# Score tiles of two attentions given the first rank in an instruction planner, and no planned distance between their steps on one engine

## The chip, the cores and the metric

The kernel runs on one core of a Trainium2 chip. A core has five engines that work side by side, each through its own instructions in a fixed order: TensorE (PE, matrix products and transposes into PSUM), VectorE (DVE), ScalarE (ACT), GpSimd (POOL), and SyncE (SP), which here issues nearly all DMAs. They wait for one another through semaphores. The metric is the device time of one execution in microseconds (us), as the median of several runs.

## The reference

One layer of a hybrid encoder on 272 tokens (16 learned meta tokens and 256 of input) of 2048 channels, in float32:

```python
hn = rmsnorm(h, mix_norm_g[l])
q_a, k_a, v_a, cq, ckv, k_pe = jnp.split(hn @ w_in[l], IN_SPLITS, axis=-1)
out_a = neighbourhood_attention(rmsnorm(q_a), rmsnorm(k_a), v_a, rpb, meta_bias)     # 8 heads of 128
out_b = mla_attention(cq, ckv, k_pe, ..., w_q_up, w_kv_up, ...)                       # 8 heads of 128 + 64
mix = jnp.concatenate([rmsnorm(out_a), rmsnorm(out_b)], axis=-1)
h = h + mix @ w_out[l]
h = h + conv_glu(rmsnorm(h), w_gate[l], w_up[l], conv_w[l], conv_b[l], w_down[l])    # width 5632
```

(The norms' gains are left out in this sketch.) Both attentions take a softmax over keys. In group A a token sees its neighbourhood on a grid and the meta tokens, with a learned bias and a mask added to the scores; in group B it sees all tokens, and queries and keys come from low-rank latents by further projections and carry a rotary part.

## The kernel before

**Precision and weights.** A float32 product is made of three products of a faster kind: each operand is split into a high and a low half, `hi = round(x)` on ACT and `lo = x - hi` on DVE. All weights pass through this: a DMA on SP brings a piece of up to 1024 columns into one of five `raw` tiles, ACT writes `whi`, DVE writes `wlo` (512 columns at a time), and PE multiplies by them (`mm3`, L595: three matmuls a block, lines L598 to L600). So PE, ACT and DVE all work for the stream of weights the whole time.

**Attention stage.** Heads are taken in four pairs. For each pair the weight stream on PE makes, in the order of `ORDERS`, the latent attention's queries and keys (Q, K), the neighbourhood attention's queries and keys (q, k), and the values of both (V, v), into four PSUM banks called `acc`. Around it other work runs: `na_queries`, `na_keys`, `na_values` and their `mla_` counterparts read those banks (which frees them), normalise and split; when queries and keys of a head are there, `na_head` (L1228) or `mla_head` (L1444) starts two *score tiles* of 128 queries by 272 keys each, `na_tile` (L1177) or `mla_tile` (L1389), 32 in all. A tile's steps are:

- score matmuls on PE (three, or five with the rotary part) into one of two PSUM banks `sps`;
- neighbourhood: scale and bias on DVE (STT, which frees the bank), row maximum on DVE (RED, L261); latent: row maximum on DVE, its product with the query's scale on DVE (`cols<-cols,rq`);
- exponential with row sum on ACT (`p<-...`; in the latent attention this frees the bank);
- reciprocal (L265) and normalisation (L249) on DVE, a copy of the 16 meta columns on ACT and its low half on DVE (`p<-p`);
- three transposes on PE into one of two banks `tps` (L287), which ACT and DVE split into `pt`.

The head then multiplies by the values (`attend`, L1020). Key sums of squares, small sums and `attend` take banks of `sps` too. After the fourth pair come the output projection and the gated MLP.

**The planner.** The order of the instructions on each engine is found when the program is built, by a list scheduler, `Flow` (L105). All work is written as threads, Python generators that yield the engine and an estimated cost of each step, wait for an `Event`, or ask for tiles from `Slots` (first come, first served). `Flow.run` (L187) again and again takes, of all threads' next steps, the one with the least

```python
key = (start, th.order(), th.seq)      # start = max(clock[eng], th.t + latency(th, eng))
```

and emits its instructions. `th.t` is when the thread's previous step ends by the plan. So the rank (`order`, the thread's `prio`, or its value when it is a function) decides among steps with one start, as all have that wait for a busy engine; less is earlier. `latency` (L114) is the distance planned between two steps of a thread: 700 to 1000 ns towards PE (`TO_PE`, `SMALL_PE`), 200 from it, 140 otherwise (`OTHER`). It is 0 where both steps are PE's, and, for threads whose `prio` is a function or at least 2, where both are on one engine. Threads are started by `fl.spawn(gen, prio=0)` (L127). The weight stream on PE has rank 1, the halves of the weights rank 2 (-1 while fewer than two pieces are ready), and nearly all others 0, among which the one spawned first goes first.

The chip's engines keep the planned order, while real times differ from the plan: an instruction whose operands are late holds up all behind it on its engine.

Of the kernel before, what the change touches and what calls it, by code (L numbers as in the profile page):

```python
# [83 lines left out]
class Event:  # L84
    def __init__(self):
        self.time, self.waiting, self.src = None, [], None
# [6 lines left out]
        self.free, self.waiting = [(0.0, t) for t in tiles], []  # L93


class Thread:
    def __init__(self, gen, t, prio, seq):
        self.gen, self.t, self.eng, self.prio, self.seq, self.req = gen, t, None, prio, seq, None
# [6 lines left out]
class Flow:  # L105
# [8 lines left out]
    def latency(self, th, eng):  # L114
        if th.eng == eng and (eng == "pe" or callable(th.prio) or th.prio >= 2):
            return 0.0
        if eng == "pe":
            if th.src == "pool":
                return self.POOL_PE
            return self.SMALL_PE if th.prio == 0 and not self.crowded else self.TO_PE  # L120
        return self.FROM_PE if th.eng == "pe" else self.OTHER

    def __init__(self):
# [85 lines left out]
def encoder_block(ctx: ExitStack, tc: tile.TileContext, io):  # L209
    nc = tc.nc  # L210
    ctx.enter_context(tc.manual_schedule())
    fl = Flow()
# [24 lines left out]
    def ACT(out, in_, f, **kw):  # L237
        ns = (51 if in_psum(in_) else 93) + 0.833 * size(in_)
        ns += 93 * (columns(kw.get("scale")) + columns(kw.get("bias")) > 0)
        yield "act", ns + 113 * ("accum_out" in kw)  # L240
        nc.scalar.activation(out, in_, f, **kw)  # L241

    def TT(out, a, b, op):
        yield "dve", 68 + 1.04 * size(out)
        nc.vector.tensor_tensor(out, a, b, op)  # L245

    def TS(out, a, s0, s1, *ops):
        yield "dve", 68 + 62 * columns(s0, s1) + (1.04 if in_psum(a) else 0.52) * size(out)
        nc.vector.tensor_scalar(out, a, s0, s1, *ops)  # L249

    def STT(out, a, s, b, op0, op1):
        yield "dve", 68 + 62 * columns(s) + 1.04 * size(out)
        nc.vector.scalar_tensor_tensor(out, a, s, b, op0, op1)  # L253
# [5 lines left out]
    def RED(out, a, op, **kw):  # L259
        yield "dve", 68 + 1.04 * size(a)  # L260
        nc.vector.tensor_reduce(out, a, AX.X, op, **kw)  # L261

    def RECIP(out, a):
        yield "dve", 75
        nc.vector.reciprocal(out, a)  # L265
# [11 lines left out]
    def MM(items):  # L277

        yield "pe", sum(cost(l, r) for _, l, r, _, _ in items)
        for o, l, r, start, stop in items:  # L280
            nc.tensor.matmul(o, l, r, start=start, stop=stop)  # L281
# [7 lines left out]
    def meta_copies(row, lo, n=P):  # L289

        out = row[:n, L : L + 3 * CW].rearrange("p (i x) -> p i x", i=3)[:, :, :N_META]
        src = row[:n, SEQ:L]
        his = out[:, :2] if lo == 2 else out[:, ::2]
        yield from ACT(his.bitcast(F32R), repeated(src, 2), AF.Copy)
        yield from TT(out[:, lo].bitcast(F32R), src, out[:, 0], ALU.subtract)
# [4 lines left out]
    def one(slots):  # L300
        (t,) = yield slots, 1
        return t
# [182 lines left out]
    def load(out, src, ev, queue):  # L485

        nc_bytes = 4 * P * size(out)
        t = max(dma_free[0], fl.cur.t) + nc_bytes / (290.0 if fl.crowded else 350.0)
        dma_free[0] = t
        queue.dma_start(out, src)  # L490
        fl.set(ev, t + (2200.0 if fl.crowded else 2000.0) - fl.cur.t)
# [504 lines left out]
    def product3(out, ls, rs, start, stop):  # L996
        (lh, ll), (rh, rl) = ls, rs
        return [(out, lh, rh, start, False), (out, lh, rl, False, False), (out, ll, rh, False, stop)]
# [13 lines left out]
    def p_transposed(p, PT, q0):  # L1012
        pt = yield from one(tps)
        yield from chunks_transposed(p, pt)
        fl.put(probs, p)
        src = pt[:, : 3 * P].rearrange("p (c q) -> p c q", c=3)
        yield from split_chunks(PT[:, :, q0 : q0 + P], src)
        fl.put(tps, pt)
# [158 lines left out]
    def na_tile(s, c, i, B, PT, done):  # L1177
        sb = yield from one(scr)
        w = yield from one(cols)
        S = yield from one(sps)  # L1180
        q0 = i * P
        k, q = s.k[c], slice(q0, q0 + P)
        yield from MM(
            product3(
                S[:, :L], (s.q[:, c, 0, q], s.q[:, c, 1, q]), (k[:, 0], k[:, 1]), True, True
            )
        )
        j = 2 * c + i
        yield from STT(sb[:, :L], S[:, :L], s.rq[:, j : j + 1], B[:, i, :], ALU.mult, ALU.add)
        fl.put(sps, S)  # L1190
        yield from RED(w[:, 0:1], sb[:, :L], ALU.max, negate=True)
        p = yield from one(probs)
        yield from ACT(p[:, :L], sb[:, :L], AF.Exp, bias=w[:, 0:1], accum_out=w[:, 1:2])
        fl.put(scr, sb)
        yield from RECIP(w[:, 2:3], w[:, 1:2])
        yield from TS(p[:, :L], p[:, :L], w[:, 2:3], None, ALU.mult)
        fl.put(cols, w)
        yield from meta_copies(p, 1)
        yield from p_transposed(p, PT[:, c], q0)
        fl.set(done)  # L1200
# [27 lines left out]
    def na_head(s, pr, c):  # L1228
        h = 2 * pr + c
        B = yield from one(bias)  # L1230
        yield "sp", 600
        ev_B = Event()
        load(B, io["na_bias"][h], ev_B, nc.sync)
        yield s.ev_q
        yield s.ev_k[c]
        yield ev_B
        if c == 0:
            s.PT = yield from one(pts)
            fl.set(s.ev_PT)
        yield s.ev_PT  # L1240
        done = [Event() for _ in range(2)]
        for i in range(2):
            fl.spawn(na_tile(s, c, i, B, s.PT, done[i]))
        if c == 1:
            fl.spawn(na_small(s, pr, s.PT, s.ev_few))
        for ev in done:
            yield ev
        fl.put(bias, B)
        yield s.ev_few
        fl.put(na_k, s.k[c])  # L1250
        s.left += 1
        if s.left == 2:
            fl.put(na_q, s.q)
            fl.put(qss, s.qs)
            fl.put(rq6, s.rq)
        yield s.ev_v[c]
        if h:
            yield ev_oa[h - 1]
        yield from attend(s.V[c], s.PT[:, c], SEQ, "g_oa", h, oa[h], sum_a, ev_oa[h])
        fl.put(na_v, s.V[c])  # L1260
        if c == 1:
            fl.put(pts, s.PT)
# [126 lines left out]
    def mla_tile(s, c, i, PT, done):  # L1389
        w = yield from one(cols)  # L1390
        p = yield from one(probs)
        S = yield from one(sps)
        S_ = S[:, :L]
        q0 = i * P
        q = slice(q0, q0 + P)
        k, kp = s.k[c], s.kp[c]
        yield from MM(
            product3(S_, (s.q[:, c, 0, q], s.q[:, c, 1, q]), (k[:, 0, :], k[:, 1, :]), True, False)
            + [(S_, s.qr[:, c, 0, q], kp, False, False), (S_, s.qr[:, c, 1, q], kp, False, True)]
        )  # L1400
        j = 2 * c + i
        rq = s.rq[:, j : j + 1]
        yield from RED(w[:, 0:1], S_, ALU.max, negate=True)
        yield from TT(w[:, 3:4], w[:, 0:1], rq, ALU.mult)
        yield from ACT(p[:, :L], S_, AF.Exp, bias=w[:, 3:4], scale=rq, accum_out=w[:, 1:2])
        fl.put(sps, S)
        yield from RECIP(w[:, 2:3], w[:, 1:2])
        yield from TS(p[:, :L], p[:, :L], w[:, 2:3], None, ALU.mult)
        fl.put(cols, w)
        yield from meta_copies(p, 1)  # L1410
        yield from p_transposed(p, PT[:, c], q0)
        fl.set(done)
# [31 lines left out]
    def mla_head(s, pr, c):  # L1444
        h = 2 * pr + c
        yield s.ev_q
        yield s.ev_qr
        yield s.ev_k[c]
        if c == 0:
            s.PT = yield from one(pts)  # L1450
            fl.set(s.ev_PT)
        yield s.ev_PT
        done = [Event() for _ in range(2)]
        for i in range(2):
            fl.spawn(mla_tile(s, c, i, s.PT, done[i]))
        if c == 1:
            fl.spawn(mla_small(s, s.PT, s.ev_few))
        for ev in done:
            yield ev
        yield s.ev_few  # L1460
        fl.put(mk, s.k[c])
        fl.put(mkp, s.kp[c])
        s.left += 1
        if s.left == 2:
            fl.put(mq, s.q)
            fl.put(mqr, s.qr)
            fl.put(qss, s.qs)
            fl.put(rq6, s.rq)
        yield s.ev_v
        if h:  # L1470
            yield ev_ob[h - 1]
        d = slice(c * P, (c + 1) * P)
        yield from attend(s.V[:, :, d], s.PT[:, c], NT, "g_ob", h, ob[h], sum_b, ev_ob[h])
        s.left_v += 1
        if s.left_v == 2:
            fl.put(mv, s.V)
            fl.put(pts, s.PT)
# [713 lines left out]
```

## Time and profile before

| | |
|---|---|
| median of 3 runs | 1108.5 us (1107.95 to 1108.92) |
| profiled execution | 1108.39 us |
| its span, first to last instruction | 1106.6 us |
| busy: PE, DVE, ACT, POOL | 1099.4, 1000.6, 726.9, 171.5 us |
| granted TensorE clock | 1.000 |
| attention tiles at work | about 84 to 284 us |

A busy engine is one with an instruction in execution. Matmuls overlap one another, so their durations add up to more than the busy time; how far apart two of them start tells what one costs. Waits in square brackets name the instruction whose semaphore came last. Lines like L245 (`TT`) or L241 (`ACT`) are those of helpers, so instructions are told apart by the tiles that they write and read.

### The profile page before, as it was taken

The numbers are of one execution on the slowest core, as the hardware profiler recorded it, in microseconds if no ns is written. First come the engines' busy times: TensorE is split into PE (matmuls) and PEld (weight loads), VectorE is DVE, ScalarE is ACT, GpSimd is POOL, SyncE is SP. The second block draws the span as 40 slices with busy tenths as digits, with TensorE's granted clock in tenths as the row PEclk, the third lists the DMA queues.
The fourth block names the chain that finished last, engine by engine and source line by source line (L and its number), as shares of the span: only waits on it lengthen the run. The fifth ranks groups of instructions, "written<-read, shape, count | busy, mean of one in ns | idle before, by whom it ended". The sixth has DMA issues, their size and how long they took to land.

```text
span 1106.6 us, 21912 instructions
## 1 busy us (share of the span) xinstructions
PE 1099.4 (99%) x8044; PEld 1045.0 (94%) x8044; DVE 1000.6 (90%) x1915; ACT 726.9 (66%) x1466; POOL 171.5 (16%) x176
## 2 busy tenths in 40 slices
PE   9999999999999999999999999999999999999998
PEld 9999999999999999999999999999999888888888
DVE  8879988999878989899999999989989999999995
ACT  8688989797647766565566565566556565665563
POOL 3210112020224301201211121120010000000003
PEclk9999999999999999999999999999999999999999
DMA  9553535353655885786767669578578877767782
GB/s 331 179 184 115 169 115 168 116 169 132 212 177 185 287 295 205 275 290 249 267 229 304 241 236 344 188 266 295 213 256 311 332 270 259 273 238 252 271 287 76
DMA packets 77603, 256.14 MB, mean 231 GB/s; under 512 B 8632, under 2 KB 14008, under 8 KB 77496
## 3 DMA queue, kind: packets, MB, share of 16 engines
q1 hardware_dynamic: 77208, 254.48, 65.5%
q8 instruction: 63, 1.03, 0.4%
q14 instruction: 44, 0.36, 0.1%
q10 hardware_dynamic: 288, 0.26, 0.1%
HBM read 234.12 MB, written 19.92 MB: 230 GB/s over the span
## 4 chain that ended last, share of the span: by engine, by line
PE 86%; DVE 8%; ACT 3%; DMA 1%; issue 1%; SPq 0%; ACTq 0%; DVEq 0%
PE bank L281 20%; PE bank L600 14%; PE bank L598 14%; PE bank L599 14%; PE bank L1855 14%; PE bank L1856 7%; DVE wlo L245 3%; PE bank L287 2%; DMA scr<-scr 1%; ACT whi L241 1%; DVE scr L253 1%; DVE mt L245 1%; ACT scr L241 1%; DVE pair L245 0%; DVE cols L261 0%
## 5 line engine op out<-in xcount | busy, mean ns | idle before, releaser
L245 DVE TENSOR_TENSOR wlo<-raw,whi 128x512 fp32r<-128x512 f32 (+2 forms) x360 | 350.0, 985 | 25.9 <-ACT whi L241 22.0
L241 ACT ACTIVATE whi<-raw 128x512 fp32r<-128x512 f32 (+2 forms) x361 | 287.9, 807 | 102.2 <-PE bank L599 45.8
L598 PE MATMUL bank<-hl,whi 128*128 128x258 f32 (+1 forms) x1216 | 349.3, 287 | 0.0
L600 PE MATMUL bank<-hl,wlo 128*128 128x258 f32 (+1 forms) x1216 | 347.4, 286 | 0.0
L599 PE MATMUL bank<-hl,whi 128*128 128x258 f32 (+1 forms) x1216 | 345.5, 284 | 0.0
L598 PEld LDWEIGHTS bank<-hl,whi 128*128 128x128 f32 x1216 | 230.8, 190 | 0.8 <-ACT whi L241 0.3
L599 PEld LDWEIGHTS bank<-hl,whi 128*128 128x128 f32 x1216 | 231.0, 190 | 0.1
L600 PEld LDWEIGHTS bank<-hl,wlo 128*128 128x128 f32 x1216 | 230.9, 190 | 0.1
L1855 PE MATMUL bank<-hl,whi 128*128 128x512 f32 x384 | 135.9, 395 | 0.0
L281 PE MATMUL bank<-whi,sin 128*128 128x256 f32 (+1 forms) x496 | 131.9, 321 | 0.0
L269 POOL TENSOR_TENSOR mt<-mt,s 128x256 f32<-128x256 f32 x44 | 66.8, 1535 | 412.9 <-ACT mt L241 411.3
L241 ACT ACTIVATE whi<-quarters 128x1024 fp32r<-128x1024 f32 x88 | 81.2, 950 | 66.0 <-PE bank L1855 45.9
L241 ACT ACTIVATE whi<-pair 128x512 fp32r<-128x512 f32 (+2 forms) x120 | 80.1, 693 | 59.2 <-DVE pair L245 45.4
L1855 PE MATMUL bank<-act,whi 128*128 128x512 f32 x308 | 109.2, 394 | 0.0
L1856 PE MATMUL bank<-hl,wlo 128*128 128x256 f32 x384 | 107.8, 281 | 0.0
L245 DVE TENSOR_TENSOR wlo<-quarters,whi 128x1024 fp32r<-128x1024 f32 x88 | 95.4, 1105 | 12.8 <-ACT whi L241 12.2
L245 DVE TENSOR_TENSOR wlo<-pair,whi 128x512 fp32r<-128x512 f32 (+2 forms) x120 | 93.2, 800 | 14.2 <-ACT whi L241 13.5
L281 PEld LDWEIGHTS bank<-whi,sin 128*128 128x128 f32 x496 | 87.8, 188 | 8.4
L1855 PEld LDWEIGHTS bank<-hl,whi 128*128 128x128 f32 x384 | 72.1, 188 | 15.1
L1856 PE MATMUL bank<-act,wlo 128*128 128x256 f32 x308 | 86.3, 280 | 0.0
L281 PE MATMUL bank<-wlo,sin 128*128 128x256 f32 (+1 forms) x248 | 79.7, 322 | 0.6 <-DVE wlo L245 0.6
L1856 PEld LDWEIGHTS bank<-hl,wlo 128*128 128x128 f32 x384 | 72.4, 189 | 0.0
(273 smaller groups left out, 2130.1 us busy)
## 6 DMA issues: line engine op xcount, KB each, us to landing
raw<-in_w_gate SPq DMA_DIRECT2D x78, 512.0 KB, 6.9
raw<-in_w_in SPq DMA_DIRECT2D x52, 512.0 KB, 4.0
quarters<-in_w_down_s SPq DMA_DIRECT2D x44, 512.0 KB, 6.9
sin<-s_up SPq DMA_DIRECT2D x40, 512.0 KB, 4.0
pair<-in_w_up_s SPq DMA_DIRECT2D x40, 512.0 KB, 5.3
raw<-in_w_down SPq DMA_DIRECT2D x40, 512.0 KB, 5.8
raw<-in_w_up SPq DMA_DIRECT2D x37, 512.0 KB, 6.8
raw<-in_w_out SPq DMA_DIRECT2D x32, 512.0 KB, 3.8
```

Of the source, the lines that this page charges most:

```text
L241: nc.scalar.activation(out, in_, f, **kw)
L245: nc.vector.tensor_tensor(out, a, b, op)
L253: nc.vector.scalar_tensor_tensor(out, a, s, b, op0, op1)
L269: nc.gpsimd.tensor_tensor(out, a, b, op)
L281: nc.tensor.matmul(o, l, r, start=start, stop=stop)
L287: nc.tensor.transpose(o, i, ident[:n, :n])
L598: nc.tensor.matmul(ps, whi, xhi, start=start, stop=False)
L599: nc.tensor.matmul(ps, whi, xlo, start=False, stop=False)
L600: nc.tensor.matmul(ps, wlo, xhi, start=False, stop=stop)
L1855: nc.tensor.matmul(ps, whi, x, start=start, stop=False)
L1856: nc.tensor.matmul(ps[:, :n], wlo, x[:, 0, :], start=False, stop=stop)
```

## The change

The two places that start score tiles give them the function `FIRST` as `prio`. It returns -1, which ranks them ahead of threads with 0, of the weight stream, and level with the weight halves at their most urgent (these were spawned earlier and win a tie). Since `prio` is now a function, `latency` also gives 0 instead of 140 ns between two steps of a tile on one engine. The distance to PE is kept at 1000 ns in the attention stage by naming `FIRST` in that condition. The small tiles of the meta queries (`na_small`, `mla_small`) and all other threads keep their rank.

```diff
+def FIRST():
+    return -1
+
+
 class Thread:
...
         if eng == "pe":
             if th.src == "pool":
                 return self.POOL_PE
-            return self.SMALL_PE if th.prio == 0 and not self.crowded else self.TO_PE
+            return self.SMALL_PE if th.prio in (0, FIRST) and not self.crowded else self.TO_PE
...
         for i in range(2):
-            fl.spawn(na_tile(s, c, i, B, s.PT, done[i]))
+            fl.spawn(na_tile(s, c, i, B, s.PT, done[i]), FIRST)
...
         for i in range(2):
-            fl.spawn(mla_tile(s, c, i, s.PT, done[i]))
+            fl.spawn(mla_tile(s, c, i, s.PT, done[i]), FIRST)
```

In the changed kernel every line from `class Thread` on stands four lines further down.

## The prediction

> **What bounds the kernel now.** I read the page first: its busy shares say which engine could set the end.
>
> ```profile
> span 1106.6 us, 21912 instructions
> PE 1099.4 (99%) x8044; PEld 1045.0 (94%) x8044; DVE 1000.6 (90%) x1915; ACT 726.9 (66%) x1466; POOL 171.5 (16%) x176
> ```
>
> TensorE (PE) is idle for 7.2 us of 1106.6. The change adds and removes no instruction, so PE's work stays and only its idle time can move. Where that idle time lies is told by busy times per stretch (columns: stretch, its length, PE, PEld, DVE, ACT, POOL, granted clock, DMA share, GB/s). The stretches go by the lives of the tiles, whose row maxima and reciprocals run from 84.1 to 283.7 us (instruction, count, least, median and greatest ns, first and last start):
>
> ```profile
> L261 DVE TENSOR_REDUCE cols<-bank x16: 422/434/436, 84.1 to 256.2; 128x1 f32<-128x272 f32 x16
> L265 DVE RECIPROCAL cols<-cols x40: 140/149/165, 86.8 to 283.7; 128x1 f32<-128x1 f32 x32, 4x1 f32<-4x1 f32 x8
> ```
>
> ```profile
> core 0: us, PE busy (x) PEld busy (x) DVE busy (x) ACT busy (x) POOL busy (x), PEclk, DMA share, GB/s
> 0.00:84.00 84.00, 82.80 (x647) 81.57 (x648) 68.88 (x146) 66.31 (x171) 23.25 (x48) 1.00 0.66 228
> 84.00:142.00 58.00, 57.11 (x470) 55.92 (x470) 54.61 (x169) 51.40 (x165) 6.09 (x10) 1.00 0.43 140
> 142.00:200.00 58.00, 57.33 (x476) 56.74 (x476) 52.33 (x153) 49.68 (x159) 10.93 (x12) 1.00 0.44 144
> 200.00:258.00 58.00, 57.72 (x480) 57.15 (x479) 52.53 (x147) 49.82 (x156) 8.36 (x12) 1.00 0.43 140
> 258.00:300.00 42.00, 42.00 (x350) 41.79 (x349) 37.51 (x95) 30.92 (x85) 6.60 (x8) 1.00 0.56 182
> 300.00:1106.60 806.60, 802.48 (x5631) 751.79 (x5630) 734.76 (x1209) 478.82 (x734) 116.31 (x87) 1.00 0.71 254
> ```
>
> From 84 to 300 us, where the tiles live, PE idles 0.89 + 0.67 + 0.28 + 0 = 1.8 us; VectorE (DVE) is busy for 197.0 of 216 us (91%), ScalarE (ACT) for 181.8. The stage is PE's, with DVE close behind. The timeline of PE shows where those 1.8 us are (start, length, instruction, idle time and what ended it):
>
> ```profile
> 85.59 0.28 PE L600 MATMUL bank<-hl,wlo 128*128 128x272 f32 x1
> 86.33 0.52 PE L281 MATMUL bank<-nak,ones_r 128*128 128x272 f32 x2 [0.46 <-ACT p L241]
> 125.44 0.28 PE L600 MATMUL bank<-hl,wlo 128*128 128x258 f32 x1
> 126.15 0.24 PE L281 MATMUL bank<-ones_r,sq8r 128*4 128x2 f32 x4 [0.43 <-ACT scr L241]
> 191.40 0.29 PE L599 MATMUL bank<-hl,whi 128*128 128x272 f32 x1
> 191.53 0.28 PE L600 MATMUL bank<-hl,wlo 128*128 128x272 f32 x1
> 192.49 0.52 PE L281 MATMUL bank<-late,mq 128*128 128x272 f32 x2 [0.67 <-ACT p L241]
> 250.67 0.28 PE L600 MATMUL bank<-hl,wlo 128*128 128x272 f32 x1
> 251.24 0.64 PE L281 MATMUL bank<-late,mq 128*128 128x272 f32 x3 [0.28 <-ACT p L241]
> ```
>
> Undisturbed, the next matmul starts 0.13 us after its predecessor (191.40 to 191.53). Here it starts 0.74, 0.71, 0.96 and 0.57 us after: 2.98 - 4 x 0.13 = 2.5 us lost. Three of the four (0.74 + 0.96 + 0.57 - 3 x 0.13 = 1.9 us) end with "ACT p": a tile's exponential lets go of one of the two score banks, and a later score or a key sum, already at the head of PE's queue, takes it.
>
> **The change, part by part.** Nothing is removed and no instruction or DMA is added; no queue on SP or POOL is touched, since the tile threads issue nothing there. What moves are the steps of 32 tiles (16 of each attention, over four pairs of heads): on PE three or five score matmuls and three transposes, on ACT an exponential and two copies, on DVE six or seven steps.
>
> *Rank.* It decides only among steps that could start at the same planned moment, which on a full engine is nearly every choice. On the second pair of the latent attention, DVE turned to a finished score like this:
>
> ```profile
> 188.32 0.42 PE L281 MATMUL bank<-mkp,mqr 128*128 128x272 f32 x2
> 188.64 0.49 DVE L253 SCALAR_TENSOR_TENSOR scr<-scr,gains,scr 128x272 f32<-128x272 f32 x1
> 189.05 0.69 DVE L245 TENSOR_TENSOR wlo<-raw,whi 128x512 fp32r<-128x512 f32 x1
> 189.66 0.42 DVE L245 TENSOR_TENSOR naq<-qraw,naq 128x258 fp32r<-128x258 f32 x1
> 189.99 0.43 DVE L245 TENSOR_TENSOR late<-scr,late 128x272 fp32r<-128x272 f32 x1
> 190.34 0.43 DVE L261 TENSOR_REDUCE cols<-bank 128x1 f32<-128x272 f32 x1
> ```
>
> The maxima of both tiles begin 1.6 us or more after their matmuls have ended (188.32 + 0.42 = 188.74 to 190.34), behind key and query work. With the rank, two tiles' DVE work (reductions 0.35 each by their spacing, smaller steps) goes ahead of it, and keys, queries and values come up to 1.6 us later. That alone I cost at nothing: the PE instructions that wait for either side are placed by the same plan, so they move along, and weight matmuls, always ready, fill the places; were they not, each pair would lose those 1.6 us. Next to be late would be the bank that a value or query thread hands back to the projections; its price is under the rivals.
>
> *No distance.* Until now a tile's step planned right behind its own predecessor on DVE or ACT was put 140 ns later, so that the planner could set a foreign step between. Now it is put directly behind. There are two such pairs of steps in each tile, all on DVE: scale-and-bias to maximum (one attention) or maximum to its product (the other), and reciprocal to normalisation. What the chip does with them:
>
> ```profile
> 190.70 0.43 DVE L245 TENSOR_TENSOR scr<-kr,scr 128x272 f32<-128x272 f32 x1
> 191.04 0.15 DVE L245 TENSOR_TENSOR cols<-cols,rq 128x1 f32<-128x1 f32 x1
> 194.92 0.43 DVE L261 TENSOR_REDUCE cols<-bank 128x1 f32<-128x272 f32 x1
> 195.39 0.16 DVE L245 TENSOR_TENSOR cols<-cols,rq 128x1 f32<-128x1 f32 x1
> 192.47 0.17 DVE L265 RECIPROCAL cols<-cols 128x1 f32<-128x1 f32 x1
> 192.66 0.36 DVE L249 TENSOR_SCALAR p<-p,cols 128x272 f32<-128x272 f32 x1
> 193.78 0.16 DVE L257 CAST sq8r<-sq 128x4 fp32r<-128x4 f32 x1
> 193.85 0.17 DVE L245 TENSOR_TENSOR p<-p 128x16 fp32r<-128x16 f32 x1
> 191.78 0.56 ACT L241 ACTIVATE p<-bank,cols,rq 128x272 f32<-128x272 f32 x1
> ```
>
> A 272-wide maximum lets an unrelated step start after 0.36 us (190.34 to 190.70), its own dependant after 0.47 (194.92 to 195.39): 0.11 more. A reciprocal is followed by its dependant after 0.19 (192.47 to 192.66); an unrelated small step follows another after 0.07 (193.78 to 193.85): 0.12 more. So a dependent pair back to back leaves DVE idle for 0.12 us, which the old 0.14 covered and the new plan does not know of. For scale-and-bias to maximum I take the same 0.12.
>
> The Trainium skill speaks against any such price: "VectorE: DVE Perf Modes", section "The DRAIN you can't avoid", reports a row of copies equally long with a semaphore after each and only after the last, and says that the semaphore costs nothing extra. By that rule the term below is zero and the sum is the profiled 1108.4. The rows above differ (0.47 against 0.36), and I go by them.
>
> How much of it reaches PE? In each pair of heads the third and the fourth latent score need the banks of the first two, and behind each bank stands one maximum-to-product pair before the exponential (190.34, 191.04, 191.78). PE now expects that exponential 0.14 earlier behind its maximum than before, while on the chip the pair takes its 0.47 all the same. At 192.49 and 251.24 there is no slack left; so 2 x 0.12 a pair, 4 x 0.24 = **0.96 us**. Bounds: from below -1.9 us (the three waits on a tile's exponential vanish, since the step at 190.70 that stood inside the first tile's pair would no longer hold it up by 0.34, and the 1.6 us of queue go); from above 32 pairs of the maximum kind x 0.12 = 3.8 us, if every one is handed on to PE. Reciprocal pairs as at 192.47 stand back to back already, so they add little; all 64 at full price would be 7.7. I take 0.96, nearer to zero, because only the bank handovers are without slack.
>
> The other attention's tiles hand over with some room, and so do the transposes:
>
> ```profile
> 194.84 0.17 DVE L245 TENSOR_TENSOR p<-p 128x16 fp32r<-128x16 f32 x1
> 195.16 0.38 PE L287 MATMUL bank<-ident,p 128*128 128x128 f32 x2
> ```
>
> The row is written by 195.01, the transpose starts at 195.16: 0.15 of room, more than one new bubble; I cost these at nothing, 0.96 at most (4 x 2 x 0.12).
>
> **Sum.** The profiled execution took 1108.39 us, its span of 1106.6 and 1.8 around it, 0.1 under the median of the three runs (1108.5). 1108.39 + 0.96 = 1109.35; on the median's footing 1109.4.
>
> **Rivals.**
> Slower: the lag on DVE is passed to PE in full. Place: score banks and transposes between 84 and 300 us; price: 0.12 for each of the 32 maximum pairs, 3.8 us, giving 1112.2. It decides once the lag of a group of tiles passes the 0.15 of room at the transposes, that is with the second bubble in a row. For it: DVE is at 91%, with 19 us idle in 216 us to catch up. Against: each PE wait sets PE back against the plan too, and so pays once for all that follows in that group.
>
> Slower by another way: values now behind tiles hand back their projection bank late.
>
> ```profile
> 166.37 0.42 DVE L245 TENSOR_TENSOR p<-bank,s 128x272 f32<-128x272 f32 x1
> 167.74 0.42 DVE L245 TENSOR_TENSOR p<-bank,s 128x272 f32<-128x272 f32 x1
> ```
>
> These two free banks just where the next pair's short projections want them. One 0.4 us step in front, at four such changes of pair, is 1.6 us: 1108.4 + 1.6 = 1110.0, or 1111.0 on top of the 0.96. Against it: by then the tiles have mostly small steps left.
>
> Faster: scores no longer wait in DVE's queue, and all four PE waits go: 1108.4 - 2.5 = 1105.9. For it: three of them end with a tile's exponential. Against: the plan also moves the waiting matmul forward, so the wait may move along; and one of the four ends with another thread's step. Nothing else in the stage can be won, for PE has only 1.8 idle us there.
>
> The change does little: the rank changes few decisions, waits as before: 1108.4. Against it: the 1.6 us of queue.
>
> **Chances.** Forecast 0.50 (its own range 1107.0 to 1110.7); slower by DVE's lag 0.19, by banks 0.08; faster 0.15; little 0.08. About 0.2% (2.2 us) is what a measurement of this kernel can tell from no change, so the bounds are 1106.3 and 1110.7: faster 0.15, same 0.50 + 0.08 = 0.58, slower 0.27. The range goes from 1106.0, the faster case's 1105.9 nearly, to 1113.0, which takes in 1112.2 and part of the 7.7; about 0.1 is left out at either end.
>
> **What would show it.** DVE: after each maximum its product, after each reciprocal its normalisation, at 0.47 and 0.19 us, without a foreign step between; maxima within 0.5 us of the end of their scores. PE: idle time between 84 and 300 us near 2.8 us instead of 1.8, at third and fourth latent scores, ended by "ACT p". After 300 us PE's idle 4.1 us (806.60 - 802.48) should stay. PE waiting for weight halves (wlo) or for projection banks, or idle time over 4 us in the tiles' stage, would make the forecast wrong upward; under 0.3 us, downward.

## The result and the profile after

The changed kernel takes 1116.5 us in the median, against 1108.5 for the kernel before: a ratio of 1.0071, with a 95% interval of 1.0058 to 1.0085. One of its six executions ran at a granted clock of 0.753 and took 1325 us, and the ratio leaves it out (median of the other five: 1116.3 us). The forecast was 1109.4, no change; the time lies 3.5 us above the range. The profiled execution took 1115.5 us, with a span of 1113.7, 7.1 us more than before. The page's head and busy shares, after:

```profile
span 1113.7 us, 21920 instructions
PE 1103.6 (99%) x8044; PEld 1044.3 (94%) x8044; DVE 1004.6 (90%) x1915; ACT 727.7 (65%) x1466; POOL 170.0 (15%) x176
```

The work is the same, 8044 matmuls and 1915 steps on DVE. Busy times by the stretches of the prediction, after (length, PE, PEld, DVE, ACT, POOL, clock, DMA share, GB/s):

```profile
0.00:84.00 84.00, 82.47 (x647) 80.72 (x648) 68.79 (x147) 66.11 (x170) 23.22 (x48) 1.00 0.65 228
84.00:142.00 58.00, 56.58 (x448) 53.58 (x447) 54.59 (x160) 49.33 (x158) 5.86 (x10) 1.00 0.39 133
142.00:200.00 58.00, 56.94 (x465) 55.46 (x466) 51.78 (x147) 49.12 (x156) 9.19 (x12) 1.00 0.42 141
200.00:258.00 58.00, 57.27 (x471) 55.97 (x470) 51.53 (x141) 49.12 (x154) 7.76 (x12) 1.00 0.42 141
258.00:300.00 42.00, 40.72 (x333) 39.55 (x333) 38.14 (x108) 31.91 (x92) 4.10 (x5) 1.00 0.49 166
300.00:1113.70 813.70, 809.60 (x5691) 759.05 (x5689) 739.77 (x1216) 482.10 (x740) 119.86 (x89) 1.00 0.71 253
```

From 84 to 300 us PE starts 448 + 465 + 471 + 333 = 1717 matmuls; before it started 1776 in the same time. At 0.12 to 0.13 us from start to start, 59 matmuls are 7.1 to 7.7 us, the whole loss. After 300 us PE idles 4.1 us, as before. So the loss is made where the tiles live, and nowhere else. Setting each weight block's start beside the same block's before shows how. Of blocks that both plans put at the same time, one is 0.1 us ahead at 84 us (in the kernel before), and later ones are behind by 1.9 at 119, 2.8 at 163, 3.6 at 185, 5.1 at 260, 7.1 from 290 us on, and then unchanged.

PE's busy time fell by only 2.6 us in those 216 us (214.15 to 211.51); the weight loads' fell by 7.0 (211.60 to 204.56). "Perfetto Trace Analysis" in the Trainium skill, section "Identifying the Most-Contended Engine", warns that matmul busy time is no good measure of the distance from the peak and takes the MFU (the share of the peak rate reached) and the busy time of the weight loads instead. The trace agrees on the weight loads: 7.0 against a loss of 7.1.

Groups of PE's instructions from 84 to 300 us (last column: idle us before them and what ended it). The scores and the transposes of the tiles, before:

```profile
L281 PE MATMUL bank<-late,mq 128*128 128x272 f32 x42 | 7.9, 297 | 1.0 <-ACT p L241 1.0
L287 PE MATMUL bank<-ident,p 128*128 128x128 f32 x136 | 21.8, 273 | 0.0
```

The same two and the other groups with more than 0.1 us of idle time, after:

```profile
L291 PE MATMUL bank<-ident,p 128*128 128x128 f32 x136 | 24.2, 278 | 1.8 <-DVE p L249 1.3 <-DVE p L253 0.5
L285 PE MATMUL bank<-late,mq 128*128 128x272 f32 x42 | 7.8, 294 | 0.1
L285 PE MATMUL bank<-late,qs 128*36 128x272 f32 (+1 forms) x16 | 3.2, 287 | 0.5 <-ACT p L245 0.5
L285 PE MATMUL bank<-late,ones_r 128*128 128x272 f32 x12 | 3.0, 317 | 0.3 <-ACT whi L245 0.3
L285 PE MATMUL bank<-ones_r,sq8r 128*4 128x2 f32 x18 | 1.5, 166 | 0.4 <-DVE sq8r L249 0.4
L285 PE MATMUL bank<-sum_b,consts 128*128 128x258 f32 x2 | 0.7, 418 | 1.2 <-DVE scr L257 1.2
```

The score matmuls (`late,mq`), at which the prediction put its loss, wait less than before (0.1 us for 1.0). The transposes (`ident,p`), which had no idle time, now have the most, and wait for DVE. One such place, on DVE:

```profile
192.60 0.68 DVE L249 TENSOR_TENSOR wlo<-raw,whi 128x512 fp32r<-128x512 f32 x1
193.20 0.43 DVE L265 TENSOR_REDUCE cols<-bank 128x1 f32<-128x272 f32 x1
193.66 0.16 DVE L249 TENSOR_TENSOR cols<-cols,rq 128x1 f32<-128x1 f32 x1
193.74 0.43 DVE L265 TENSOR_REDUCE cols<-bank 128x1 f32<-128x272 f32 x1
194.21 0.16 DVE L249 TENSOR_TENSOR cols<-cols,rq 128x1 f32<-128x1 f32 x1
194.29 0.44 DVE L249 TENSOR_TENSOR late<-scr,late 128x272 fp32r<-128x272 f32 x1
194.64 0.16 DVE L269 RECIPROCAL cols<-cols 128x1 f32<-128x1 f32 x1
194.83 0.36 DVE L253 TENSOR_SCALAR p<-p,cols 128x272 f32<-128x272 f32 x1
195.11 0.43 DVE L249 TENSOR_TENSOR scr<-kr,scr 128x272 f32<-128x272 f32 x1
195.46 0.15 DVE L269 RECIPROCAL cols<-cols 128x1 f32<-128x1 f32 x1
195.65 0.36 DVE L253 TENSOR_SCALAR p<-p,cols 128x272 f32<-128x272 f32 x1
195.93 0.17 DVE L249 TENSOR_TENSOR p<-p 128x16 fp32r<-128x16 f32 x1
```

and on PE:

```profile
191.17 0.42 PE L285 MATMUL bank<-mkp,mqr 128*128 128x272 f32 x2
...
194.75 0.28 PE L604 MATMUL bank<-hl,wlo 128*128 128x272 f32 x1
195.25 0.44 PE L291 MATMUL bank<-ident,p 128*128 128x128 f32 x2 [0.21 <-DVE p L253]
196.15 0.33 PE L291 MATMUL bank<-ident,p 128*128 128x128 f32 x1 [0.46 <-DVE p L249]
```

Each maximum is followed at 0.46 to 0.47 us by its product, each reciprocal at 0.19 by its normalisation, nothing between: the pairs are as the change plans them. Of the 64 pairs (two in each tile), 21 stood directly together on DVE before, 57 do now. But the maxima still start 1.6 us or more after their scores have ended (191.17 + 0.42 to 193.20), and PE stands at the transposes: the first of them starts 0.50 us after the weight matmul ahead of it (undisturbed 0.13), when the normalised rows are there, and the third 0.90 us after the first, when the last step on DVE has ended.

**How far each engine is behind the plan.** The planner's own starts for every step (from running the kernel's planner) can be set beside the starts in the trace. Median lag in us (traced start less planned start) of the steps planned in the 6 us from the time at the head of the column, which is planned time:

```
                         66      84     126     180     240     288
before          DVE     1.4     3.4     4.5     5.7     6.5     5.6
                PE      1.4     2.2     3.5     4.0     5.2     5.9
after           DVE     1.3     4.0     6.7     9.4    11.7    12.8
                PE      1.3     2.6     5.2     7.6     9.7    13.1
```

By plan PE ends at the same time in both kernels, 1096.36 us, and from 84 to 286 us it has no planned gap in either. All of the loss is lag: 13.1 - 5.9 = 7.2 us. DVE falls behind, and PE, given about 1 us of room, is drawn along.

Step by step, the same comparison shows where DVE's lag is made. Between planned 84 and 290 us it grows by 8.9 us in the changed kernel and by 2.2 in the kernel before. The pairs of a tile that stand directly together make 6.4 of the 8.9 us; before they made -0.3. All other steps on DVE make 2.5 us in both. In such a pair a normalisation is planned 0.075 us behind the start of its reciprocal and starts 0.19 behind it; before it was planned 0.215 behind and started 0.20 behind. Over the whole run the 57 pairs lose 6.8 us against the plan, 0.12 each.

### The profile page after: what moved, and what is told of

Its sections match the earlier page's. It is cut to its first block, busy times and chain, and to the rows that moved or that the text cites. A ratio compares the mean times of both kernels' runs of the same rounds, so it can differ in the third digit from the quotient of the medians.

```text
span 1113.7 us, 21920 instructions
## 1 busy us (share of the span) xinstructions
PE 1103.6 (99%) x8044; PEld 1044.3 (94%) x8044; DVE 1004.6 (90%) x1915; ACT 727.7 (65%) x1466; POOL 170.0 (15%) x176
## 4 chain that ended last, share of the span: by engine, by line
PE 84%; DVE 10%; ACT 4%; issue 1%; DMA 1%; SPq 0%; DVEq 0%; ACTq 0%
PE bank L285 20%; PE bank L604 14%; PE bank L603 14%; PE bank L602 14%; PE bank L1859 14%; PE bank L1860 7%; DVE wlo L249 3%; PE bank L291 1%; ACT whi L245 1%; DVE scr L257 1%; DVE cols L265 1%; DVE p L253 1%; DVE mt L249 1%; ACT scr L245 1%; DMA scr<-scr 0%
## 5 line engine op out<-in xcount | busy, mean ns | idle before, releaser
L249 DVE TENSOR_TENSOR wlo<-quarters,whi 128x1024 fp32r<-128x1024 f32 x88 | 95.3, 1105 | 12.8 <-ACT whi L245 12.2
```

## The experiments

Two theories. *Lag*: the 0.12 us that DVE idles between a step and its dependant is not in the new plan; DVE falls behind, and PE meets results that are not there. *Rank*: keys, queries and values behind the tiles are late, and PE waits for those.

All times below are set beside the kernel before as it ran in the same session (1108.6 to 1108.8 us); on that footing the change costs 7.9 us.

**The change's two halves, each alone.** The lines shown are edits of the changed kernel.

```diff
 # rank alone: the distance again
-        if th.eng == eng and (eng == "pe" or callable(th.prio) or th.prio >= 2):
+        if th.eng == eng and (eng == "pe" or th.prio is not FIRST and (callable(th.prio) or th.prio >= 2)):
 # distance of zero alone: the rank as before
 def FIRST():
-    return -1
+    return 0
```

> The change with its rank kept and its distance undone: the tiles rank at -1, but 140 ns are planned again between two of their steps on DVE. Theory lag (the 0.12 us that a dependent pair leaves DVE idle is unknown to the plan, DVE falls behind it, PE comes to the transposes too early): the loss goes, 1107.5 to 1110. Theory rank (keys, queries and values are late behind the tiles, and what PE does for them waits): the loss stays, 1114 to 1118.

> The change with its distance of zero kept and its rank undone: the tiles rank at 0 like the others, as before, with nothing planned between two steps on one engine. Theory lag: most of the loss stays, 1112 to 1117, with the dependent pairs back to back and PE waiting at transposes. Theory rank: 1107.5 to 1110.

Rank alone: 1109.8 us, ratio 1.0013 (1.0004 to 1.0023). No distance alone: 1114.0, ratio 1.0048 (1.0033 to 1.0063). Both lie in the ranges of the lag theory. So the missing distance costs 5.4 of the 7.9 us by itself, the rank 1.2. Together they cost 1.3 more than the sum. With the rank 57 pairs stand together, without it 46, since foreign steps of rank 0 still come between; eleven pairs at 0.12 us are 1.3 us. The rank's 1.2 us alone is mostly the plan's own: with it alone the planned end comes 0.9 us later, with 0.9 us of planned gaps on PE. The plan of the whole change has no such gap, so beside the missing distance the rank costs its 2.5 us (1116.5 less 1114.0) in another way, of which the eleven pairs explain about half. Two of the groups on PE with the rank alone:

```profile
L602 PE MATMUL bank<-late,whi 128*128 128x258 f32 (+1 forms) x48 | 14.5, 302 | 0.4 <-ACT qraw L245 0.4
L285 PE MATMUL bank<-late,mq 128*128 128x272 f32 x42 | 7.8, 295 | 0.6 <-ACT p L245 0.6
```

The 0.4 us ahead of a projection, ended when a query had been read out of its bank (`qraw`), is a wait for a projection bank, which the prediction had as a rival; the rival named values where this is a query, and priced it at 1.6 us, four times as much.

**The idle time put into the plan.** Rank and distance are as in the change, but the planner knows the 120 ns. A second run has the same with rank 0.

```diff
+            if eng == "dve" and th.prio is FIRST and th.eng == eng and start == th.t:
+                cost += 120.0
             th.t = self.clock[eng] = start + cost
```

> The changed kernel whose plan counts 120 ns more for a tile's step on DVE that follows its own predecessor directly, so that the idle time of the pair is in the plan; rank -1, no foreign step between. Theory lag: PE's instructions move behind by as much as DVE really needs, the waits at transposes go, 1107.5 to 1110.5. Theory rank: 1114 to 1118, since the order among threads is nearly that of the change.

> Distance zero without the rank, and the plan counts 120 ns for a tile's step on DVE directly behind its own predecessor: beside the run of the distance alone (1114.0) only the plan's knowledge of the idle time differs. Theory lag: at least three quarters of those 5.4 us go, 1108 to 1110. Theory order (it is the other order of DVE's steps, pairs together instead of interleaved, that costs, whatever the plan believes): 1112 to 1115.

With the rank: 1110.8 us, ratio 1.0020 (1.0010 to 1.0030), 0.3 us above the lag theory's range, though 60 pairs now stand together. Of the 7.9 us 5.7 are gone while the chip does the same pairs; PE's lag at 288 us falls from 13.1 to 7.6. Without the rank: 1110.6, ratio 1.0017 (1.0008 to 1.0027). That is 3.4 of 5.4 us gone instead of three quarters, between the ranges of the two theories and nearer to lag; here 1.1 us are in the plan's end. So most of the cost is not that the pairs stand together and idle, but that the plan does not know of it. The runs do not hold all else equal: with other costs the planner puts other steps on DVE in another order, too.

**More room towards PE.** The changed kernel with 1800 instead of 1000 ns to a tile's step on PE.

```diff
-            return self.SMALL_PE if th.prio in (0, FIRST) and not self.crowded else self.TO_PE
+            if th.prio is FIRST and not self.crowded:
+                return self.SMALL_PE + 800.0
+            return self.SMALL_PE if th.prio == 0 and not self.crowded else self.TO_PE
```

> The changed kernel with 1800 instead of 1000 ns planned from a tile's step on another engine to its step on PE. Theory lag: PE has weight matmuls to do in the 0.8 us that DVE is behind, so the waits at the tiles' transposes and scores shrink and most of the loss goes, 1108 to 1111. Theory rank: the waits of keys, small sums and group sums are not touched, 1113 to 1118.

1113.4 us, ratio 1.0042 (1.0027 to 1.0057): outside the lag theory's range and inside that of rank. Where PE waits tells what happened. PE's groups with the most idle time, 84 to 300 us, in this run:

```profile
L293 PE MATMUL bank<-ident,qraw 128*128 128x128 f32 x30 | 4.8, 274 | 0.4 <-DVE pt L251 0.4
L287 PE MATMUL bank<-late,qs 128*36 128x272 f32 (+1 forms) x16 | 3.1, 287 | 0.7 <-ACT p L247 0.7
L287 PE MATMUL bank<-late,ones_r 128*128 128x272 f32 x12 | 2.6, 301 | 0.8 <-ACT oa L247 0.8
L287 PE MATMUL bank<-ones_r,sq8r 128*4 128x2 f32 x18 | 1.5, 165 | 1.9 <-DVE p L255 0.9 <-ACT scr L247 0.4 <-DVE sq8r L251 0.2
```

The tiles' transposes are gone from the list, but key sums, small sums (0.4 us before, 1.9 now) and the queries' transposes have taken their place. DVE runs in one order, so its lag is everyone's: giving room to the tiles alone moves the waits to the threads that kept 1000 ns. DVE's lag has not gone: PE's lag at 288 us is still 11.5 us, against 13.1. The expectation of the lag theory had overlooked that the other threads' steps stand in the same late queue. The run by itself does not tell lag from rank.

**One attention at a time.** `FIRST` given at one of the two places only.

```diff
 # neighbourhood alone
-            fl.spawn(mla_tile(s, c, i, s.PT, done[i]), FIRST)
+            fl.spawn(mla_tile(s, c, i, s.PT, done[i]))
 # latent alone
-            fl.spawn(na_tile(s, c, i, B, s.PT, done[i]), FIRST)
+            fl.spawn(na_tile(s, c, i, B, s.PT, done[i]))
```

> The change for the neighbourhood attention's 16 tiles alone. The prediction costed their half at nothing, 0.96 us at most: 1108 to 1109.5. Theory lag with both halves handing their lag to PE at the transposes: 1110.5 to 1113, half of the 7.9 us.

> The change for the latent attention's 16 tiles alone. The prediction put the whole loss of 0.96 us here: 1109 to 1110. Theory lag: half or more of the 7.9 us, 1111.5 to 1114, with waits at the transposes.

1110.4 (ratio 1.0015, 1.0005 to 1.0024) and 1111.3 us (1.0026, 1.0015 to 1.0037). Neither half costs what either theory said: 1.6 + 2.5 = 4.1 of 7.9 us. The neighbourhood's half is not free, and of its 1.6 us 1.05 lie in a plan that ends later. The pairs that stand together lose 3.3 us against the plan in one run and 3.45 in the other, together as much as the 6.8 of the whole change, but not all of it reaches PE. At 288 us PE's lag is 3.0 us above that of the kernel before with the latent half, and only 1.3 above it with the neighbourhood's. That fits a DVE which regains ground in the other attention's stretch; no run shows it directly.

**Lag in the kernel before.** DVE falls 4.2 us further behind there too, from 1.4 at 66 us to 5.6 at 288. Two cures: more room to PE for all threads of rank 0, or a dearer step on DVE in the plan, by 8 and by 14 ns in the attention stage. The lines shown are edits of the kernel before.

```diff
 # more room
-    SHARED, SMALL_PE = 0.2, 1000.0
+    SHARED, SMALL_PE = 0.2, 1300.0
 # a dearer step (8.0, and 14.0 in another run)
+            if eng == "dve" and not self.crowded:
+                cost += 8.0
             th.t = self.clock[eng] = start + cost
```

> The kernel before with 1300 instead of 1000 ns planned towards PE in the attention stage, for all its threads of rank 0: room against DVE's lag everywhere. If lag is also what makes the four waits of the kernel before (2.5 us), they shrink: 1106 to 1108. If work that comes later to PE is itself what the banks wait for, it loses more than it gains: 1109 to 1112.

> The kernel before whose plan counts 8 ns more for every step on DVE in the attention stage. There DVE falls 4.2 us further behind its plan over some 560 steps, 7.5 ns a step (before: planned starts set beside the trace's). Theory lag: with this in the plan the lag stops growing and the four PE waits of 2.5 us shrink: 1106 to 1108.5. If the four waits come from single late steps and not from the lag: 1108.5 to 1110.

> As the run of the kernel before with 8 ns more for every DVE step in the attention stage (1108.1), but 14 ns more: with 8, DVE still fell 2.9 us further behind its plan. Theory lag: a little more goes, 1106 to 1108. If what is left has another cause: 1108 to 1110.

More room: 1109.9 us, ratio 1.0010 (1.0000 to 1.0020), no gain: its plan ends 2.5 us later, at 1098.81, though PE's lag at 288 us falls to 4.6. A dearer step: 1108.1 (0.9992, 0.9983 to 1.0001) with 8 ns, which can't be told from no change, and 1106.65 us (0.9979, 0.9970 to 0.9988) with 14 ns, which beats both kernels, though by plan it ends 0.9 us later. DVE's lag is then 1.6 us at 66 us, 3.6 at 126 and 2.4 at 288. The busy times from 84 to 300 us, of the kernel before and of this run:

```profile
84.00:300.00 216.00, 214.15 (x1770) 211.60 (x1770) 196.98 (x561) 181.81 (x563) 31.98 (x42) 1.00 0.46 149
84.00:300.00 216.00, 215.98 (x1793) 214.00 (x1792) 197.74 (x564) 183.53 (x565) 28.96 (x43) 1.00 0.46 151
```

PE idles 0.02 us for 1.85, and starts 1793 matmuls for 1770: the four waits of the prediction are gone. (In one window of 216 us the view counts 1770 for the kernel before; its four stretches above add up to 1776.)

**The change with both corrections**, the 120 ns of the pairs and 8 ns a step:

```diff
+            if eng == "dve" and th.prio is FIRST and th.eng == eng and start == th.t:
+                cost += 120.0
+            if eng == "dve" and not self.crowded:
+                cost += 8.0
             th.t = self.clock[eng] = start + cost
```

> The run with the planned idle time of 120 ns (1110.8, rank -1) and also 8 ns more for every step on DVE in the attention stage. Theory lag: what is left of its loss, 2.2 us, is DVE's remaining lag and shrinks: 1107 to 1109.5. If the rest is the rank's own: 1109.5 to 1111.5.

1109.6 us, ratio 1.0006 (0.9997 to 1.0015): not told from the kernel before. It lies just inside the range named for a rest that is the rank's own, and 0.1 us above that of the lag theory. Beside the kernel before with the same 8 ns (1108.1) 1.5 us are left. They are lag and not planned gaps, since by plan PE ends 0.3 us earlier here (1097.12) than there (1097.39); which steps make them is not shown.

## Why the prediction was wrong

*The price of a pair was right.* It is 0.47 and 0.19 us, as forecast, and scale-and-bias to maximum, for which 0.12 was taken by analogy, measures 0.52 where an unrelated step follows after 0.41:

```profile
283.81 0.49 DVE L257 SCALAR_TENSOR_TENSOR scr<-bank,rq,bias 128x272 f32<-128x272 f32 x1
284.33 0.43 DVE L265 TENSOR_REDUCE cols<-scr 128x1 f32<-128x272 f32 x1
```

The 0.41 is from two such steps of different tiles in a row before the change, 0.90 us together, of which the second takes 0.49:

```profile
157.36 0.90 DVE L253 SCALAR_TENSOR_TENSOR scr<-bank,rq,bias 128x272 f32<-128x272 f32 x2
```

The rule of the Trainium skill set against it, in "VectorE: DVE Perf Modes", section "The DRAIN you can't avoid", gave zero and 1108.4 us. For the steps of this kernel the run with the distance alone taken away (1114.0 us) speaks against it as the rows did; no run here repeats the row of copies that the page reports.

*The step that failed is "How much of it reaches PE?"*, the term of 0.96 us, 7.1 in the trace. It counted 8 pairs, at two score banks a pair of heads, and costed transposes and the other attention at nothing, because they had 0.15 us of room, "more than one new bubble". That treated each handover by itself. Room is used up once; the lag adds up over the stage, since PE's plan has no gap to give it back in. The table of lags shows it: DVE goes from 1.3 to 12.8 us, PE follows 1 to 2 us behind for most of the stage, and hardly anything is regained between two pairs of heads.

*The ceiling was too low, for a reason of its own.* The prediction took "32 pairs of the maximum kind x 0.12 = 3.8", because the reciprocal pairs "stand back to back already, so they add little". On the chip 18 of the 32 did. But their normalisation was planned 0.215 us behind the reciprocal's start, which covered the 0.20 it took, and is now planned 0.075 behind. What the chip does at such a pair is unchanged, and the lag is new all the same. So the price falls on all 57 pairs that stand together, not only on the 36 that newly do: 6.8 us, against 7.1 in the trace. The 7.7 for "all 64 at full price", named and set aside, was near. Knowing the 0.12 takes 5.5 us off PE's lag in the run with the rank; what makes up the rest there is not shown.

*The slower rival named the mechanism* (DVE's lag handed to PE in full, at score banks and transposes, decided by the second bubble in a row), with a chance of 0.19 and 1112.2 us. The argument against it, that a wait of PE "pays once for all that follows in that group", is what the table of lags refutes: PE's lag grows from each pair of heads to the next. Its price of 3.8 us was still too low, for the same reason as the ceiling.

*The rank was costed at nothing*; it costs 1.2 us alone and 2.5 beside the missing distance, the smaller part of the change. The reason given misread a row. The 1.6 us between a score and its maximum was taken for foreign work chosen ahead, which the rank would jump. By plan, the median wait in the latent attention was 0.7 us, and 0.4 with the rank; in the trace it was 1.65 and is 1.85. More than half of that queue was lag, and the rank moves a step in the plan, not the lag. For the same reason "maxima within 0.5 us of the end of their scores" did not come true. The faster rival rested on the same reading and fell with it.

*The signs to look for worked.* Idle time over 4 us in the tiles' stage was named as what would make the forecast wrong upward: it is 1.42 + 1.06 + 0.73 + 1.28 = 4.5. Banks of the projections showed as 0.4 us in the run with the rank alone.

## What to carry to other kernels

Where an order of instructions is planned and one engine's plan is full, ask of each edit not what it does to the waits that the trace shows, but how far it lets the plan's prices depart from the chip's: a small price that the plan does not know adds up over the whole stage and comes out as waits elsewhere. Price every place whose plan the edit touches, also those where the chip will do just what it did. Set planned and traced starts side by side before blaming rank or order; here that pointed to prices, and 14 ns on each planned DVE step gained 0.2% where the change of rank and distance had lost 0.7%. Read PE's loss from started matmuls or from the weight loads' busy time, since its own busy time showed only 2.6 of 7.1 us.

## What the runs showed of the hardware that was not expected

A step on DVE that needs its predecessor's result starts 0.11 to 0.12 us later than an unrelated one, for a maximum (0.47 for 0.35), a reciprocal (0.19 for 0.07) and a scale-and-bias (0.53 for 0.41) alike, so over these three the extra time does not go by the size of the step. The figures are medians from start to start: of 15, 31 and 11 dependent pairs in the changed kernel, and of 30, 14 and 15 tile steps that an unrelated step followed in the kernel before. And DVE's busy share of 91% in the stage was no sign of time to catch up in: with 20 us of it free by the profile (216 - 196.0), the changed kernel did not make up 7 us of lag in 200.
